# Where the activations' region lies in SBUF: allocated beside xs, at the same remainder modulo 512 bytes

## The chip, the cores and the metric

The kernel runs on one core of a Trainium2 chip. The metric is the device time of one execution in microseconds (us). Runs are compared by their median; the kernel before takes 947.79 us (three runs, 947.37 to 948.18).

## The reference, cut to what matters

A two-layer encoder trunk works on x, 256 positions by 1024 features, in float32. Each layer runs a SwiGLU block, a mixer and a second SwiGLU block, each behind an RMS norm and added back to x:

```python
def swiglu(h, w_gu, w_down):
    g, u = jnp.split(h @ w_gu, 2, axis=-1)
    return (jax.nn.silu(g) * u) @ w_down

for l in range(DEPTH):                     # DEPTH = 2, D_MODEL = 1024, D_FF = 2816
    x = x + 0.5 * swiglu(rmsnorm(x, ffn1_norm[l]), ffn1_w_gu[l], ffn1_w_down[l])
    ...                                    # mix: gated MLP and differential attention, or MLA and GQA
    x = x + mix
    x = x + 0.5 * swiglu(rmsnorm(x, ffn2_norm[l]), ffn2_w_gu[l], ffn2_w_down[l])
```

The four SwiGLU blocks hold most of the arithmetic: per block a gate-and-up product (1024 to 2 x 2816) and a down product (2816 to 1024).

## The kernel before

Features lie along the 128 partitions, positions along the free axis. Every float32 operand of the large products is cut into two float32r parts, a high part and the remainder (hi and lo). A 1 MB piece of weights is loaded by DMA into one of four raw tiles; ScalarE (or VectorE) copies it to a hi tile and VectorE subtracts to make the lo tile. There are six hi and six lo tiles of 1024 elements a partition, used in turn.

Three groups of activations live in SBUF for the products:

- **xs** (KT x 2 x N elements, 8 x 2 x 256): the normed input, hi part (256 columns) and lo part (256 columns) side by side for each of the eight slices of 128 features. Written by `scaled`, read by the gate-and-up products and by the mixers' input products.
- **region** (11264 elements a partition): in a SwiGLU block it holds hs, the 22 slices of the activations, again 256 columns hi and 256 columns lo each (`hs = Arena(region)(FT, 2, N)`). In a mixer it holds the mixer's output os_ and the transposed queries and keys.
- **region32** (5472 elements a partition): float32 intermediates of the mixers.

Two shapes of product do most of the work. In `wide`, a pair of matmuls, the weights are stationary and the activations move: 512 columns (hi and lo) against the hi weights, then 256 columns (hi alone) against the lo weights.

```python
c = T.matmul(b, lhsT=wh, rhs=flat(x2), start=first, stop=False)
c += T.matmul(b[:, 1, :], lhsT=wl, rhs=x2[:, 0, :], start=False, stop=last)
```

The gate-and-up loop runs `wide` over xs with four PSUM banks in rotation (two pairs of gate and up). The down loop runs `wide` over hs in region with two banks in turn: for the last block, the seventh output slice has one bank, and the eighth slice goes through `dense` instead. `dense` is three matmuls (hi with hi, hi with lo, lo with hi). In `out_product`, the mixers' output product, and in that eighth slice, the moving operand of `dense` is 256 columns of region. In `block`, the mixers' input product, the roles are turned: 128 columns of xs are stationary and up to 512 columns of weights move.

The order of all instructions is chosen once, while the kernel is built, by a list scheduler (`Program.schedule`) from costs and dependencies; dependencies are kept by tile name and offset within a tile. Where a tile lies in SBUF is no input to it. Tiles are placed by the pool in the order in which `keep` is called. In the built program the byte addresses within a partition are:

| tile | start before | modulo 512 | start after | modulo 512 |
|---|---|---|---|---|
| hi, lo (all twelve) | 76928 to 121984 | 128 | the same | 128 |
| region | 126080 | 128 | 157984 | 288 |
| region32 | 171136 | 128 | 126080 | 128 |
| gx | 193024 | 0 | 147968 | 0 |
| ident, ones, onesr | 201472 to 202496 | 256 | 156416 to 157440 | 256 |
| xs | 203040 | 288 | 203040 | 288 |

A slice of hs or xs is 2048 bytes, the lo half starts 1024 bytes into it, and 128 columns of weights are 512 bytes, so every operand of `wide` begins at the same remainder modulo 512 as its tile.

Of the kernel before, what the change touches and what calls it, by code (L numbers as in the profile page):

```python
# [12 lines left out]
F32R = mybir.dt.float32r  # L13
# [8 lines left out]
N = 256  # L22
KT = D // P
# [12 lines left out]
ARENA, ARENA32 = 11264, 5472  # L36
# [315 lines left out]
def trunk_kernel(ctx: ExitStack, tc: tile.TileContext, a: dict, out: bass.AP):  # L352
# [20 lines left out]
    def keep(nm, *shape, dt=F32):  # L373
        return sb.tile([P, *shape], dt, name=nm)
# [40 lines left out]
    banks = [ps.tile([P, 512], F32, name=f"bank{k}") for k in range(8)]  # L415
    bank = Taken("bank", Kind(banks, SPARE, True, MOST[0]))
    aux = Taken("aux", Kind(banks, SPARE, True, MOST[1]))
    region, region32 = keep("region", ARENA, dt=F32R), keep("region32", ARENA32)

    def flat(z):  # L420
        return z.rearrange("p a b -> p (a b)")
# [142 lines left out]
        return tp[:w]  # L564


    xs = keep("xs", KT, 2, N, dt=F32R)
    rr_, rb, acc, acc2 = keep("rr", 2), keep("rb", N), keep("acc", N), keep("acc2", 2, N, dt=F32R)
    rr = [rr_[:, h:h + 1] for h in range(2)]

# [587 lines left out]
```

## Time and profile before

| | |
|---|---|
| median of three runs | 947.79 us |
| the profiled execution's own time | 947.75 us |
| its span, from the first to the last instruction | 946.0 us |
| TensorE matmul (PE), busy | 939.6 us, 99% of the span |
| VectorE (DVE), busy | 724.0 us, 77% |
| ScalarE (ACT), busy | 548.4 us, 58% |
| granted TensorE clock | 1.000 |

Every instruction is recorded through one helper, so all lines read L285; the groups are told apart by tiles. A matmul's row names out<-moving,stationary: `bank<-region,hi` streams columns of region past hi weights. Buffer numbers are left out, so region32 is shown as region too; the float32r forms with hi and lo are region's alone. The times of matmuls overlap: the modelled end of one lies behind the start of the next, so the pace of a stream is read from the starts of its instructions, not from their mean durations.

### The profile page before, as it was taken

To read this page: it belongs to the slowest core of one execution; us is meant where nothing else is said; L and a number is where in the kernel's file an instruction comes from. 1 tells how busy PE (TensorE), PEld (TensorE's weight loads), DVE (VectorE), ACT (ScalarE), POOL (GpSimd) and SP (SyncE) were. 2 spreads that over 40 slices of the span, in tenths; PEclk is the share of its full clock that TensorE was granted. 3 is DMA by queue.
4 is the path that set the end of the run, shared out by engine and by line. 5 is a ranking of instruction groups with operands and counts; after the bars stand their busy time and mean duration, and the time that the engine had idled before them with its cause. 6 is when DMAs were issued, how large, how long until landed. Compare 5 with 4: busy or idle time off the path is not lost.

```text
span 946.0 us, 14528 instructions
## 1 busy us (share of the span) xinstructions
PE 939.6 (99%) x5564; PEld 827.1 (87%) x5564; DVE 724.0 (77%) x1326; ACT 548.4 (58%) x938; POOL 29.4 (3%) x57
## 2 busy tenths in 40 slices
PE   9999999999999999999999999999999999999998
PEld 8888888888899888888888888888989988888887
DVE  7997776579989878866588887756888698887642
ACT  7765655446856656554465656544587566565430
POOL 0920000000000000000000000000000000000000
PEclk9999999999999999999999999999999999999999
DMA  8675555543355555555555555554412355555520
GB/s 334 258 267 178 188 201 191 178 178 134 106 207 177 184 193 203 178 182 191 195 182 187 185 202 192 178 185 162 178 55 85 110 186 196 180 192 205 191 102 22
DMA packets 26422, 167.83 MB, mean 177 GB/s; under 512 B 2929, under 2 KB 5105, under 8 KB 7025
## 3 DMA queue, kind: packets, MB, share of 16 engines
q1 hardware_dynamic: 26352, 166.92, 50.0%
q8 instruction: 43, 0.70, 0.3%
q14 instruction: 27, 0.21, 0.1%
HBM read 165.86 MB, written 1.05 MB: 176 GB/s over the span
## 4 chain that ended last, share of the span: by engine, by line
PE 97%; DVE 1%; ACT 1%; DMA 0%; issue 0%; SPq 0%; ACTq 0%
PE bank L285 97%; DVE t L285 0%; ACT t L285 0%; DMA raw<-in_gu 0%; DVE sm L285 0%; ACT hi L285 0%; DVE region L285 0%; DVE lo L285 0%; ACT L285 0%; DVE hi L285 0%; DVE ssg L285 0%; DVE gx L285 0%; SPq L285 0%; DVE ssc L285 0%; DVE rc L285 0%
## 5 line engine op out<-in xcount | busy, mean ns | idle before, releaser
L285 DVE TENSOR_TENSOR lo<-raw,hi 128x1024 fp32r<-128x1024 f32 (+2 forms) x318 | 382.4, 1204 | 165.9 <-ACT hi L285 161.0
L285 ACT ACTIVATE hi<-raw 128x1024 fp32r<-128x1024 f32 (+3 forms) x310 | 322.6, 1043 | 306.1 <-PE bank L285 193.2
L285 PE MATMUL bank<-xs,hi 128*128 128x512 f32 x1408 | 490.8, 393 | 0.4 <-ACT hi L285 0.4
L285 PE MATMUL bank<-xs,lo 128*128 128x256 f32 x1408 | 394.8, 280 | 0.0
L285 PEld LDWEIGHTS bank<-xs,hi 128*128 128x128 f32 x1408 | 265.4, 189 | 59.1 <-ACT hi L285 0.7
L285 PE MATMUL bank<-region,hi 128*128 128x512 f32 (+1 forms) x982 | 296.6, 364 | 0.0
L285 PEld LDWEIGHTS bank<-xs,lo 128*128 128x128 f32 x1408 | 265.3, 188 | 0.7 <-DVE lo L285 0.7
L285 PE MATMUL bank<-region,lo 128*128 128x256 f32 x832 | 234.0, 281 | 0.0
L285 PEld LDWEIGHTS bank<-region,hi 128*128 128x128 f32 x982 | 174.9, 189 | 32.0
L285 PEld LDWEIGHTS bank<-region,lo 128*128 128x128 f32 x832 | 157.6, 189 | 0.0
L285 ACT ACTIVATE t<-bank 128x256 f32<-128x256 f32 (+1 forms) x201 | 76.5, 400 | 39.4 <-PE bank L285 38.4
L285 PE MATMUL bank<-hi,xs 128*128 128x512 f32 (+2 forms) x256 | 78.6, 381 | 0.0
L285 DVE TENSOR_TENSOR t<-bank,t 128x256 f32<-128x256 f32 x176 | 67.3, 420 | 0.4 <-ACT t L285 0.4
L285 DVE TENSOR_TENSOR t<-t,rb 128x512 f32<-128x512 f32 x88 | 60.3, 689 | 1.2
L285 PEld LDWEIGHTS bank<-hi,xs 128*128 128x128 f32 x256 | 47.1, 188 | 8.7
L285 DVE SCALAR_TENSOR_TENSOR gx<-bank,gx 128x256 f32<-128x256 f32 (+1 forms) x71 | 28.4, 450 | 28.7 <-PE bank L285 28.6
L285 PE MATMUL bank<-lo,xs 128*128 128x512 f32 (+2 forms) x128 | 48.0, 375 | 0.0
L285 DVE TENSOR_TENSOR t<-t,t 128x256 f32<-128x256 f32 (+2 forms) x108 | 45.9, 428 | 0.1
L285 ACT ACTIVATE t<-t 128x256 f32<-128x256 f32 (+2 forms) x98 | 39.0, 406 | 3.1 <-DVE t L285 3.1
L285 DVE TENSOR_TENSOR region<-t,region 128x256 fp32r<-128x256 f32 (+2 forms) x92 | 39.1, 430 | 1.1 <-ACT region L285 1.1
L285 ACT ACTIVATE region<-t 128x256 fp32r<-128x256 f32 (+1 forms) x89 | 35.5, 404 | 1.6 <-DVE t L285 1.4
L285 ACT ACTIVATE xs<-gx 128x256 fp32r<-128x256 f32 x48 | 24.0, 500 | 10.8 <-DVE gx L285 9.7
(129 smaller groups left out, 467.4 us busy)
## 6 DMA issues: line engine op xcount, KB each, us to landing
raw<-in_gu SPq DMA_DIRECT2D x86, 1024.0 KB, 4.8
raw<-in_dn SPq DMA_DIRECT2D x44, 1024.0 KB, 4.8
raw<-in_ev_in SPq DMA_DIRECT2D x10, 1024.0 KB, 4.8
raw<-in_ev_out SPq DMA_DIRECT2D x4, 1024.0 KB, 4.9
raw<-in_od_out SPq DMA_DIRECT2D x4, 1024.0 KB, 4.7
raw<-in_gu SPq DMA_DIRECT2D x8, 256.0 KB, 4.6
raw<-in_od_q SPq DMA_DIRECT2D x2, 1024.0 KB, 5.0
raw<-in_od_c SPq DMA_DIRECT2D x2, 832.0 KB, 4.3
```

Source lines behind the costliest of these rows:

```text
L285: r = fn(*map(real, args), **{k: real(v) for k, v in kw.items()})
```

## The change

`region` is no longer allocated ahead of `region32` but just ahead of `xs`. Its size, its contents and every instruction that uses it stay; the addresses change as in the table above. On every engine the built program has the same instructions in the same order.

```diff
@@ -415,7 +415,7 @@
     bank = Taken("bank", Kind(banks, SPARE, True, MOST[0]))
     aux = Taken("aux", Kind(banks, SPARE, True, MOST[1]))
-    region, region32 = keep("region", ARENA, dt=F32R), keep("region32", ARENA32)
+    region32 = keep("region32", ARENA32)
 
     def flat(z):
@@ -564,7 +564,8 @@
         return tp[:w]
 
 
-    xs = keep("xs", KT, 2, N, dt=F32R)
+
+    region, xs = keep("region", ARENA, dt=F32R), keep("xs", KT, 2, N, dt=F32R)
     rr_, rb, acc, acc2 = keep("rr", 2), keep("rb", N), keep("acc", N), keep("acc2", 2, N, dt=F32R)
```

## Rows read from the trace of the kernel before

**Rows 1.** The page: busy time by engine, and the chain that ended last.

```profile
PE 939.6 (99%) x5564; PEld 827.1 (87%) x5564; DVE 724.0 (77%) x1326; ACT 548.4 (58%) x938; POOL 29.4 (3%) x57
...
PE 97%; DVE 1%; ACT 1%; DMA 0%; issue 0%; SPq 0%; ACTq 0%
```

**Rows 2.** Windows: four down stretches, two gate-and-up stretches, the end.

```profile
core 0: us, PE busy (x) PEld busy (x) DVE busy (x) ACT busy (x) POOL busy (x), PEclk, DMA share, GB/s
130.34:192.51 62.17, 62.17 (x354) 53.95 (x353) 38.68 (x56) 29.22 (x40) 0.00 (x0) 1.00 0.53 187
410.55:472.72 62.17, 62.17 (x354) 53.95 (x353) 38.68 (x56) 29.21 (x40) 0.00 (x0) 1.00 0.53 187
594.99:657.16 62.17, 62.17 (x354) 53.92 (x353) 38.77 (x56) 29.21 (x40) 0.00 (x0) 1.00 0.52 180
879.70:934.10 54.40, 54.40 (x311) 47.20 (x309) 28.48 (x39) 19.66 (x23) 0.00 (x0) 1.00 0.34 120
...
296.15:410.55 114.40, 114.40 (x662) 100.69 (x661) 93.43 (x154) 69.58 (x124) 0.00 (x0) 1.00 0.54 190
479.20:594.99 115.79, 115.79 (x670) 101.96 (x669) 94.00 (x153) 69.39 (x125) 0.00 (x0) 1.00 0.54 188
...
925.00:950.00 25.00, 17.18 (x119) 15.75 (x117) 3.85 (x8) 1.05 (x1) 0.00 (x0) 0.95 0.06 21
```

**Rows 3.** Groups by form on PE: out<-moving,stationary, shapes, xcount, busy us, mean ns.

```profile
L285 PE MATMUL bank<-xs,hi 128*128 128x512 f32 x1408 | 490.8, 393 | 0.4 <-ACT hi L285 0.4
L285 PE MATMUL bank<-xs,lo 128*128 128x256 f32 x1408 | 394.8, 280 | 0.0
L285 PE MATMUL bank<-region,hi 128*128 128x512 f32 x682 | 241.1, 399 | 0.0
L285 PE MATMUL bank<-region,lo 128*128 128x256 f32 x832 | 234.0, 281 | 0.0
...
L285 PE MATMUL bank<-region,hi 128*128 128x256 f32 x300 | 55.5, 286 | 0.0
...
L285 PE MATMUL bank<-region 64*128 64x256 f32 x96 | 10.2, 290 | 0.2 <-DVE region L285 0.2
```

**Rows 4.** Timeline of PE, gate-and-up: first and last of 98 pairs; start, duration.

```profile
339.83 0.39 PE L285 MATMUL bank<-xs,hi 128*128 128x512 f32 x1
...
373.80 0.39 PE L285 MATMUL bank<-xs,hi 128*128 128x512 f32 x1
```

**Rows 5.** Timeline of PE, down with two banks: first and last of 96 pairs.

```profile
414.78 0.40 PE L285 MATMUL bank<-region,hi 128*128 128x512 f32 x1
...
448.70 0.40 PE L285 MATMUL bank<-region,hi 128*128 128x512 f32 x1
```

**Rows 6.** Timeline of PE, last block's seventh slice, one bank: 21 pairs.

```profile
926.33 0.40 PE L285 MATMUL bank<-region,hi 128*128 128x512 f32 x1
...
933.75 0.40 PE L285 MATMUL bank<-region,hi 128*128 128x512 f32 x1
```

**Rows 7.** Timeline of PE, even mixer's input product: seven threes of 512 columns.

```profile
201.13 0.63 PE L285 MATMUL bank<-hi,xs 128*128 128x512 f32 x2
...
206.03 0.63 PE L285 MATMUL bank<-hi,xs 128*128 128x512 f32 x2
```

**Rows 8.** Timeline of PE, last block's eighth slice: twenty threes of 256 columns.

```profile
934.34 0.28 PE L285 MATMUL bank<-region,lo 128*128 128x256 f32 x1
...
941.54 0.28 PE L285 MATMUL bank<-region,lo 128*128 128x256 f32 x1
```

**Rows 9.** Groups by form: VectorE and ScalarE writing hs, on ScalarE the hi tiles.

```profile
L285 DVE TENSOR_TENSOR region<-t,region 128x256 fp32r<-128x256 f32 x88 | 36.7, 421 | 1.1 <-ACT region L285 1.1
L285 ACT ACTIVATE region<-t 128x256 fp32r<-128x256 f32 x87 | 34.6, 401 | 1.6 <-DVE t L285 1.4
L285 ACT ACTIVATE hi<-raw 128x1024 fp32r<-128x1024 f32 x294 | 311.0, 1060 | 295.2 <-PE bank L285 186.2 <-issue 103.2 <-ACT hi L285 2.7
```

## The prediction

> **What bounds the kernel now.** I read the page first, then the windows of single stages, then the groups by form, and last the timeline of TensorE, which carries the argument. The page shows TensorE busy 939.6 us of a 946.0 us span, and the chain that ended last lies on it for 97% [rows 1]. So nearly every nanosecond taken from the pace of the matmul stream is taken from the end. [...]
>
> The pace is not the same everywhere, and the busy share hides that. A gate-and-up step and a down step are the same pair of matmuls, 512 moving columns against hi and 256 against lo, with the same count of columns. The starts in the timeline give each one's pace. Gate-and-up moves xs: (373.80 - 339.83) / 98 = 346.6 ns a pair [rows 4]. Down moves region: (448.70 - 414.78) / 96 = 353.3 ns a pair [rows 5]. [...] The difference of 6.7 ns is small and steady, in stretches in which TensorE waits for nobody.
>
> **What differs between the two streams.** By the addresses in the built program, xs begins at remainder 288 modulo 512 and region at 128; the weights of both begin at 128. The other difference is the number of PSUM banks: four in rotation for gate-and-up, two for down. Three more stretches help to separate these.
>
> - The seventh slice of the last block runs the same pairs over region into one bank: (933.75 - 926.33) / 21 = 353.3 ns [rows 6]. Two banks or one make no difference.
> - The even mixer's input product has the roles turned: the weights (remainder 128) move, xs (288) is stationary. Seven threes take 206.03 - 201.13 = 4.90 us, 233.3 ns for one matmul of 512 columns [rows 7].
> - The last block's eighth slice moves 256 columns of region (128): twenty threes take 941.54 - 934.34 = 7.20 us, 120.0 ns for one [rows 8].
>
> The last two add up to 233.3 + 120.0 = 353.3 ns, just the pair of the down stretch, though their stationary operands lie at 288 and 128 and their banks change in other ways. So everything that moves columns from remainder 128 fits one set of prices, whatever the stationary operand and the banks. Only xs, which moves from 288, is faster. I conclude that the remainder of the moving operand sets the 6.7 ns. That is inferred from stretches that differ in more than one thing; no run here has changed the address alone.
>
> **The change part by part.** It moves tiles and no instruction, so nothing is added, removed or reordered on any engine, and no wait is new.
>
> 1. *Down pairs over region.* After the change, hs begins at 288, with the weights at 128 as before: the address remainders of the gate-and-up stream. There are 682 such pairs (the 512-column form of region with hi [rows 3]): 176 in each of three blocks, 154 in the last. I price each at the pace of xs: 682 x (353.3 - 346.6) = 682 x 6.7 = 4.57 us. By stretch that is 1.18 us off each 62.17 and 1.03 us off the 54.40 [rows 2]. All of it is on the path. What could come late instead is the feed of weights; but gate-and-up already runs at 346.6 ns with VectorE at 93.4 of 114.4 us [rows 2], and in down VectorE has more room, 38.7 of 62.2. ScalarE's 1060 ns copies of hi have most of their idle time behind TensorE (186.2 us waiting for a bank's reader to finish [rows 9]), so the tiles wait for TensorE and not the reverse.
>
> 2. *256-column matmuls of region outside the pairs.* There are 300 with hi and 832 - 682 = 150 with lo [rows 3], 450 in all, in the two output products and the eighth slice. The pair's rows do not say which of its two matmuls is the shorter from 288. One end: it is all the 256-column one, which would fall from 120.0 to 113.3 ns and give 450 x 6.7 = 3.0 us more. The other end: the 256-column one becomes dearer while the 512-column one more than pays for it. The mean durations of the forms are 393 against 399 ns for 512 columns and 280 against 281 for 256 [rows 3]: six of the seven nanoseconds sit in the 512-column matmul. A loss of 2.5 ns on each, half of what lies between the two 256-column means of region (281 and 286), would be 1.1 us. I take zero, which is nearest to the row of 280 against 281, and keep -3.0 and +1.1 for the range.
>
> 3. *The other tiles.* region32, gx, ident, ones and onesr shift by 45056 bytes, 88 x 512, so they keep their remainder. I cost them at nothing; if absolute position mattered, the eight slices of xs and the twelve weight tiles, which all lie elsewhere, would not run at one pace over 98 pairs. Region is also an operand of 96 matmuls in the mixers' attention [rows 3]; at 6.7 ns either way that is 0.6 us, and they are short, with VectorE and ScalarE work between them. I take zero.
>
> 4. *Writers.* ScalarE and VectorE write hs while TensorE reads xs, now at the same remainders. No row shows such a write slowing the stream: hi and lo tiles, at 128, are written beside region at 128 all through rows 5, with VectorE busy 38.7 of 62.2 us; in rows 6, at the end, it is busy 3.85 of 25 us and ScalarE 1.05 [rows 2]; the pace is the same. I take zero; its price is among the rivals.
>
> The sum is 4.57 us. Against the profiled execution: 946.0 - 4.6 = 941.4 us of span, with 947.75 - 946.0 = 1.75 us outside it, 943.2 us. The median, 947.79, is 0.04 above that execution, so 943.2 stands for the median too.
>
> **The rivals.**
>
> *No change (947.8 us).* The four-bank rotation, not the address, makes gate-and-up fast, and down stays at 353.3 ns. For it: the only fast stretch is also the only one with four banks changing at every pair. Against it: one and two banks cost the same [rows 5, 6], and prices from stretches with other bank patterns add up to the same pair [rows 7, 8]. [...]
>
> *Part of the gain is given back (944.6 us).* Writes of hs meet reads of xs at the same remainder. The writes take 36.7 + 34.6 = 71.3 us [rows 9]; in that time TensorE does 71.3 / 0.3466 = 206 pairs of gate-and-up, and if each falls back to 353.3 ns, 206 x 6.7 = 1.4 us of the 4.6 are lost. Against it stands point 4.
>
> *More than the sum (940.2 us).* The gain sits in the 256-column matmul, and the 450 others get it too, 3.0 us. Against it stand the durations in point 2.
>
> *Slower (956.2 us).* A start at 288, which is 32 bytes past a multiple of 64, costs TensorE time, and xs runs fast only because four banks hide more than that. Down, with two banks, then shows the cost: taking the step seen here, 6.7 ns for 512 columns and half of it for 256, it is 682 x (6.7 + 3.35) + 450 x 3.35 = 6.9 + 1.5 = 8.4 us. It decides as soon as a down pair takes more than 353.3 ns. For it: no stretch moves columns from 288 with two banks or one. Against it: the stream at 288 is the fastest here, and the banks have shown no price.
>
> **How the numbers follow.** Forecast 0.72, giving-back 0.06, more than the sum 0.07, no change 0.11, slower 0.04. The likeliest gives 943.2 us. Its own spread (point 2's small differences, point 3's 0.6, runs that differ by 0.4 either way) is about 942.2 to 944.4. The range reaches to 945.6 above, which takes in giving-back, and to 941.2 below, which takes in part of the case of 940.2; no change, slower and the rest below are left out, 0.20 together. A difference of 0.2%, 1.9 us, is about what a measurement of this kernel can tell from no change. Forecast, giving-back and more than the sum are faster by more than that: 0.85. No change is 0.11, slower 0.04.
>
> **What would show it right or wrong.** In the profile of the changed kernel the down stretches should have pairs 346.6 ns apart, so about 61.0 us instead of 62.17 and 53.4 instead of 54.40; the 512-column form of region with hi should have a mean near 393 ns. Gate-and-up pairs should stay at 346.6 (347 or more would be giving-back), the eighth slice's matmuls at 120.0 (113 would be more than the sum), the input products at 233.3. If the down pairs stay at 353.3 while region lies at 288, my reading of the remainder is wrong, and the banks are next to be tried.

## The result and the profile after

The changed kernel takes 942.35 us (median of six runs, 942.05 to 942.80) against 947.63 us for the kernel before beside it: a ratio of 0.9941, 95% interval 0.9930 to 0.9951. The forecast was 943.2 us, 4.6 us less than before; measured are 5.3 us less. The profiled execution has a span of 940.6 us instead of 946.0.

The windows of the same stretches as in [rows 2], four down and two gate-and-up, with the same columns:

```profile
130.23:191.25 61.02, 61.02 (x355) 53.73 (x354) 38.68 (x56) 29.24 (x40) 0.00 (x0) 1.00 0.55 190
408.92:469.93 61.01, 61.01 (x354) 53.72 (x353) 38.66 (x56) 29.23 (x40) 0.00 (x0) 1.00 0.53 189
592.19:653.20 61.01, 61.01 (x354) 53.73 (x353) 38.72 (x56) 29.27 (x40) 0.00 (x0) 1.00 0.53 183
875.49:928.87 53.38, 53.38 (x310) 46.99 (x309) 28.46 (x39) 19.71 (x23) 0.00 (x0) 1.00 0.35 122
294.52:408.92 114.40, 114.40 (x663) 100.73 (x661) 93.43 (x154) 69.61 (x124) 0.00 (x0) 1.00 0.55 190
476.40:592.19 115.79, 115.79 (x670) 101.98 (x669) 93.98 (x153) 69.42 (x125) 0.00 (x0) 1.00 0.54 188
```

The down stretches went from 62.17 to 61.01 us and from 54.40 to 53.38: 1.15 + 1.16 + 1.16 + 1.02 = 4.5 us. Gate-and-up has not moved by a hundredth. TensorE is as fully busy as before (61.01 of 61.01 us in the second down stretch) and the granted clock is the same, 1.00; the stream itself has become denser. The first and the last of 98 down pairs in the timeline of TensorE (start, duration), against [rows 5]:

```profile
412.73 0.39 PE L285 MATMUL bank<-region,hi 128*128 128x512 f32 x1
...
446.70 0.39 PE L285 MATMUL bank<-region,hi 128*128 128x512 f32 x1
```

(446.70 - 412.73) / 98 = 346.6 ns a pair, the pace of xs. The groups by form, against [rows 3]:

```profile
L285 PE MATMUL bank<-region,hi 128*128 128x512 f32 x682 | 236.6, 392 | 0.0
L285 PE MATMUL bank<-region,lo 128*128 128x256 f32 x832 | 232.8, 280 | 0.0
...
L285 PE MATMUL bank<-region,hi 128*128 128x256 f32 x300 | 54.8, 284 | 0.0
...
L285 PE MATMUL bank<-region 64*128 64x256 f32 x96 | 10.2, 291 | 0.2 <-DVE region L285 0.2
```

The 512-column form went from a mean of 399 to 392 ns, the mean of xs. The rest of the gain is in the 256-column matmuls outside the pairs. The eighth slice of the last block, 22 threes against the twenty of [rows 8] (the first row is the matmul just ahead of them, the last of the seventh slice):

```profile
928.76 0.28 PE L285 MATMUL bank<-region,lo 128*128 128x256 f32 x1
...
936.50 0.28 PE L285 MATMUL bank<-region,lo 128*128 128x256 f32 x1
```

That is 7.74 us / 66 = 117.3 ns instead of 120.0. The mixers' stretches, which hold the other 384 of these matmuls, in the windows of the kernel before:

```profile
192.51:288.27 95.76, 95.75 (x582) 82.68 (x581) 85.75 (x215) 63.55 (x109) 0.00 (x0) 1.00 0.44 155
657.16:757.42 100.26, 99.19 (x717) 91.48 (x715) 80.98 (x229) 67.05 (x139) 0.00 (x0) 1.00 0.31 109
```

and after:

```profile
191.25:286.64 95.39, 95.39 (x582) 82.33 (x581) 85.53 (x215) 63.36 (x108) 0.00 (x0) 1.00 0.45 155
653.20:753.22 100.02, 98.97 (x716) 91.30 (x715) 80.89 (x229) 66.94 (x139) 0.00 (x0) 1.00 0.31 109
```

They are 0.4 and 0.2 us shorter. The starts place most of the even mixer's part in the output product. Its longest unbroken stretch, 34 threes, before and after:

```profile
275.91 0.28 PE L285 MATMUL bank<-region,lo 128*128 128x256 f32 x1
...
288.15 0.28 PE L285 MATMUL bank<-region,lo 128*128 128x256 f32 x1
...
274.55 0.28 PE L285 MATMUL bank<-region,lo 128*128 128x256 f32 x1
...
286.52 0.28 PE L285 MATMUL bank<-region,lo 128*128 128x256 f32 x1
```

12.24 us became 11.97, 120.0 ns for one matmul became 117.4. In the other long stretches of the output products, read in the same way, the gain is smaller, 1.3 ns for one: fifty threes of the odd mixer went from 757.30 - 739.30 = 18.00 us to 753.11 - 735.30 = 17.81, eighteen of the even mixer from 6.48 to 6.41. With 66 x 2.7 ns = 0.2 us in the eighth slice, 4.5 + 0.6 + 0.2 = 5.3 of the 5.4 us of span are placed.

### The profile page after: what moved, and what is told of

The parts are those of the page before. It is cut to its first block, busy times and chain, and to the rows that moved or that the text cites. A ratio compares the mean times of both kernels' runs of the same rounds, so it can differ in the third digit from the quotient of the medians.

```text
span 940.6 us, 14528 instructions
## 1 busy us (share of the span) xinstructions
PE 934.3 (99%) x5564; PEld 825.5 (88%) x5564; DVE 724.2 (77%) x1326; ACT 548.2 (58%) x938; POOL 27.2 (3%) x57
## 4 chain that ended last, share of the span: by engine, by line
PE 97%; DVE 1%; ACT 1%; DMA 0%; issue 0%; SPq 0%; ACTq 0%
PE bank L285 97%; DVE t L285 0%; ACT t L285 0%; DMA raw<-in_gu 0%; DVE sm L285 0%; ACT hi L285 0%; DVE region L285 0%; DVE lo L285 0%; ACT L285 0%; DVE hi L285 0%; DVE ssg L285 0%; DVE gx L285 0%; SPq L285 0%; DVE ssc L285 0%; DVE rc L285 0%
## 5 line engine op out<-in xcount | busy, mean ns | idle before, releaser
L285 PE MATMUL bank<-region,hi 128*128 128x512 f32 (+1 forms) x982 | 291.4, 359 | 0.0
```

The lines of the kernel that those rows point to most:

```text
L285: r = fn(*map(real, args), **{k: real(v) for k, v in kw.items()})
```

## The experiments

All move tiles or the place of data within a tile; the contents and the arithmetic stay. Up to the scans each run has, on every engine, the instructions of the changed kernel in the same order, so there addresses alone differ. In the scans TensorE's order is still the same, but a few instructions of VectorE and ScalarE change places; in the versions with two starts the order shifts on TensorE too. The edits are shown against the changed kernel or the kernel before, whichever is nearer. In what follows d is the start of the moving operand minus that of the stationary operand, modulo 512 bytes. Before the change d was 160 for gate-and-up and 0 for down; the change made it 160 for both. For the mixers' input products, whose moving operand is the weights, it was 352 and stayed so. Each scan was timed once, so its trace is read and not its time.

**xs moved as well, both at 128.**

```diff
+    region, xs = keep("region", ARENA, dt=F32R), keep("xs", KT, 2, N, dt=F32R)
     region32 = keep("region32", ARENA32)
```

> region and xs both begin at remainder 128, like the weights; from the changed kernel (942.35 us) only addresses differ. Theory A (the moving operand's own start decides): gate-and-up pairs slow from 346.6 to 353.3 ns as the down pairs go back to 353.3; 1408 x 6.7 = 9.4 us and 682 x 6.7 = 4.6 us and about 0.7 us for the 450 others, together 957.1 us. Theory B (the relation of moving to stationary decides): the same here, since the difference is zero. Theory C (four banks in rotation keep gate-and-up fast and something else helped the down pairs): gate-and-up stays at 346.6, down returns to 353.3, 947.6 us.

954.88 us (three runs at 954.78 to 955.07, one at 952.28), a ratio of 1.0065 (1.0051 to 1.0080) to the kernel before. The timeline of TensorE in gate-and-up, first and last of 98 pairs, then the even mixer's input product, first and last of seven threes, then twenty threes of the last block's eighth slice:

```profile
339.67 0.40 PE L285 MATMUL bank<-xs,hi 128*128 128x512 f32 x1
...
374.30 0.40 PE L285 MATMUL bank<-xs,hi 128*128 128x512 f32 x1
...
202.83 0.62 PE L285 MATMUL bank<-hi,xs 128*128 128x512 f32 x2
...
207.59 0.61 PE L285 MATMUL bank<-hi,xs 128*128 128x512 f32 x2
...
941.57 0.28 PE L285 MATMUL bank<-region,lo 128*128 128x256 f32 x1
...
948.77 0.28 PE L285 MATMUL bank<-region,lo 128*128 128x256 f32 x1
```

Gate-and-up has 34.63 us / 98 = 353.4 ns with all four banks in rotation: the banks are out, and with them the rival of no change. But the input products, whose moving operand still lies at 128, went from 233.3 to 4.76 us / 21 = 226.7 ns. Neither theory A nor the plain form of B said that. Over the 288 matmuls of this shape (192 with hi, 96 with lo) that makes, as an estimate, 288 x 6.6 ns = 1.9 us, most of what the time is under the 957.1 expected. The eighth slice kept 7.20 us / 60 = 120.0 ns.

**The weights at 288 too.**

```diff
-    raws_, his, los = Turns("raw", RAW, SUB), Turns("hi", RING, PIECE, F32R), Turns("lo", RING, PIECE, F32R)
+    raws_ = Turns("raw", RAW, SUB)
...
     warm = keep("warm", 1)
+    his, los = Turns("hi", RING, PIECE, F32R), Turns("lo", RING, PIECE, F32R)
```

> hi and lo tiles also begin at remainder 288, with region and xs at 288: moving and stationary operands have the same remainder, none is at 128. Theory A: down and gate-and-up pairs stay at 346.6 ns, and the input products, whose moving operand is now at 288, fall from 233.3 to about 229 ns for 512 columns; 288 of those matmuls x 4 ns = 1.2 us less, 941.2 us. Theory B: equal remainders are slow, so both streams take 353.3 ns: 1408 x 6.7 + 682 x 6.7 = 14 us more, about 957 us.

950.22 us, ratio 1.0027 (1.0016 to 1.0038); its twelve runs lie in two groups, 948.3 to 948.9 and 951.5 to 952.7. So a moving start of 288 is not fast in itself (353.3 ns a pair in the first window below): theory A falls. Nor is d = 0 always slow. Its windows, a gate-and-up and a down stretch twice:

```profile
294.13:410.72 116.59, 116.59 (x663) 101.07 (x661) 93.91 (x154) 69.76 (x124) 0.00 (x0) 1.00 0.54 185
410.72:472.91 62.19, 62.19 (x355) 53.90 (x353) 38.67 (x55) 29.22 (x40) 0.00 (x0) 1.00 0.53 189
479.51:595.31 115.80, 115.80 (x671) 102.10 (x670) 93.97 (x153) 69.38 (x125) 0.00 (x0) 1.00 0.54 188
595.31:656.32 61.01, 61.01 (x355) 53.79 (x353) 38.70 (x56) 29.21 (x40) 0.00 (x0) 1.00 0.52 183
```

With 330, 176, 334 and 176 pairs these are 353.3, 353.4, 346.7 and 346.6 ns. One program with one d runs whole stretches at either pace. In both blocks of these windows the down stretch had the pace of the gate-and-up before it. Of the other two, the first block's down stretch was fast, 61.01 us / 176 = 346.6 ns, and the fourth block's gate-and-up slow: 649 matmuls in 114.00 us, against 647 in as long a window of the second block's and 660 of the third's.

**region at 256, and region at 160.** The tile warm (32 bytes) is placed behind region instead of ahead; in the second, warm and region go ahead of region32.

> region begins at 256 (a multiple of 64), xs stays at 288, the weights at 128. Theory A, in the form that multiples of 64 are slow: down pairs 353.3 ns, 947.6 us. Theory B (equality with the stationary operand's remainder is what is slow): 256 differs from 128, so down pairs stay at 346.6 ns, 942.4 us.

> region begins at 160, 32 past a multiple of 64 but not at xs's remainder modulo 512 (288); the weights stay at 128. Theory A in the form of 64 bytes: down pairs 346.6 ns, 942.4 us. If it has to be the remainder of xs modulo 512 itself: down pairs 353.3 ns, 947.6 us. Theory B by the distance from the weights: 32 is another distance than 160, anything between 346.6 and 353.3 ns.

945.84 us, ratio 0.9982 (0.9973 to 0.9991), and 941.78 us, ratio 0.9936 (0.9923 to 0.9949). The second down stretch of each in the windows, region at 256 first:

```profile
410.04:471.83 61.79, 61.79 (x355) 54.16 (x354) 38.67 (x56) 29.21 (x40) 0.00 (x0) 1.00 0.54 188
```

```profile
408.47:469.49 61.02, 61.02 (x355) 54.09 (x354) 38.66 (x56) 29.23 (x40) 0.00 (x0) 1.00 0.54 191
```

Over 176 pairs that is 351.1 ns at d = 128, between the two paces and as neither theory had it, and 346.7 at d = 32. The same remainder as xs isn't needed.

**All shifted by 32: weights at 288, region and xs at 320.** The edit is that of the run with the weights at 288, with a tile of 32 bytes behind them. Theory B2, in this expectation and the next ones, is what the runs so far left of B: the pace depends on d, and not only on whether d is zero.

> As the run with the weights at 288, but region and xs lie 32 bytes further, at 320: d = 32 for all pairs, and every moving operand of a pair starts at a multiple of 64. Theory B2: pairs 346.7 ns as in the run with region at 160 and the weights at 128, so the distance alone decides; 942 us or less. Theory A (multiples of 64 are slow): 353 ns in both streams, 957 us.

941.81 us in its one run. Gate-and-up and down in the windows:

```profile
294.35:408.76 114.41, 114.41 (x662) 101.41 (x661) 93.38 (x154) 69.57 (x124) 0.00 (x0) 1.00 0.55 190
408.76:469.77 61.01, 61.01 (x354) 54.09 (x353) 38.65 (x56) 29.22 (x40) 0.00 (x0) 1.00 0.54 190
```

346.7 and 346.6 ns with the moving operands at a multiple of 64, where theory A asked for 353. The moving operand's own start does not decide in these runs. The third block of the first scan below makes it sharper: there hs begins at 320 too, with the weights at 128 (d = 192), and its pairs take 353.3 ns. The two streams with a start of 320 differ in where the operands lie to each other. That d alone sets the pace, wherever both lie, was tried at two distances only, 0 and 32, and d = 0 has two paces, 353.3 and 346.7 ns.

**The scans.** Region gets 56 elements more, and each of the four SwiGLU blocks puts hs at another offset in it.

```diff
-        hs = Arena(region)(FT, 2, N)
+        hs = view(region[:, shift:shift + FT * 2 * N], (FT, 2, N))
...
-    ffn(*f10, norm[1])
+    ffn(*f10, norm[1], 16)
```

> A scan inside one run: the activations of the four SwiGLU blocks begin 64, 128, 192 and 224 bytes past the weights' remainder, xs 384 past it (address only; the contents are the same). Let d be the start of the moving operand minus that of the stationary one, modulo 512. Theory B2 (d decides; so far pairs took 353.3 ns at d = 0, 351.1 at 128, 346.7 at 32 and 160): pairs differ from block to block with d, the second block near 351, the fourth and perhaps the others at 346.7; the input products at d = 128 take neither 227.8 (d = 0) nor 233.5 ns (d = 352) for certain. Theory A (own start, multiples of 64 are slow): the blocks at 64, 128 and 192 past 128 are multiples of 64 and all near 353, the fourth (352) at 346.7, gate-and-up (0) at 353.

> The same scan with d = 224, 288, 352 and 384 for the four blocks and d = 128 for gate-and-up, input products at d = 384. Theory B2: gate-and-up near 351 ns as the down pairs were at d = 128 before; the blocks again by d. Theory A (multiples of 64): the first three blocks start at 352, 416 and 480, 32 past multiples of 64, so 346.7; the fourth starts at 0, so 353.

> The rest of the scan: d = 320, 416, 448 and 480 in the four blocks, gate-and-up and input products at d = 256. If the pace repeats every 256 bytes, pairs take 353.3 ns at 320 (as at 64), 346.7 at 416 (as at 160), 353.3 at 448 (as at 192), 346.7 at 480 (as at 224), and 353.3 at 256 (as at 0, with input products near 227.8). If the 512 bytes of one weight load set it, 256 is an ordinary distance and the others need not repeat.

> d = 480 again, in the first, third and fourth block, and d = 96 in the second block and in gate-and-up, with input products at d = 416. If 480 is slow by itself, all three blocks take about 353 ns a pair. If at 480 a stretch falls into one of two paces, as at 0 and 256, the three differ or take 346.7. If the pace repeats every 256 bytes, d = 96 is like 352 (350.0 ns).

The down stretches of these four runs in their windows (176 pairs in the first three of a run, 154 in the fourth). d = 64, 128, 192, 224:

```profile
131.90:194.08 62.18, 62.18 (x354) 54.23 (x353) 38.67 (x55) 29.20 (x40) 0.00 (x0) 1.00 0.53 188
413.38:475.18 61.80, 61.80 (x355) 54.18 (x354) 38.66 (x55) 29.21 (x40) 0.00 (x0) 1.00 0.53 187
598.99:661.17 62.18, 62.18 (x354) 54.01 (x353) 38.75 (x55) 29.21 (x40) 0.00 (x0) 1.00 0.52 180
885.08:938.47 53.39, 53.39 (x311) 46.92 (x309) 28.44 (x38) 19.68 (x23) 0.00 (x0) 1.00 0.35 121
```

d = 224, 288, 352, 384:

```profile
132.94:193.96 61.02, 61.02 (x354) 53.63 (x353) 38.64 (x55) 29.24 (x40) 0.00 (x0) 1.00 0.54 190
412.95:473.96 61.01, 61.01 (x354) 54.08 (x353) 38.64 (x55) 29.22 (x40) 0.00 (x0) 1.00 0.54 190
597.78:659.39 61.61, 61.61 (x355) 53.79 (x354) 38.75 (x55) 29.22 (x40) 0.00 (x0) 1.00 0.52 181
883.09:937.16 54.07, 54.07 (x310) 47.39 (x309) 28.46 (x38) 19.65 (x23) 0.00 (x0) 1.00 0.35 120
```

Two gate-and-up stretches at d = 256 (330 and 334 pairs), and down at d = 320, 416, 448, 480:

```profile
131.58:193.76 62.18, 62.18 (x354) 54.17 (x353) 38.68 (x55) 29.20 (x40) 0.00 (x0) 1.00 0.54 187
295.64:412.24 116.60, 116.60 (x663) 101.07 (x661) 93.95 (x154) 69.78 (x124) 0.00 (x0) 1.00 0.54 187
412.24:473.27 61.03, 61.03 (x355) 53.73 (x354) 38.66 (x55) 29.25 (x40) 0.00 (x0) 1.00 0.54 189
479.85:595.64 115.79, 115.79 (x670) 102.09 (x669) 93.94 (x153) 69.36 (x125) 0.00 (x0) 1.00 0.54 188
595.64:657.82 62.18, 62.18 (x355) 54.01 (x353) 38.69 (x56) 29.22 (x40) 0.00 (x0) 1.00 0.52 180
879.60:934.00 54.40, 54.40 (x311) 47.25 (x309) 28.50 (x39) 19.68 (x23) 0.00 (x0) 1.00 0.34 120
```

d = 480, 96, 480, 480:

```profile
132.14:194.32 62.18, 62.18 (x355) 54.00 (x354) 38.64 (x55) 29.19 (x40) 0.00 (x0) 1.00 0.54 187
413.49:475.09 61.60, 61.60 (x354) 53.66 (x353) 38.64 (x55) 29.21 (x40) 0.00 (x0) 1.00 0.54 188
598.56:660.74 62.18, 62.18 (x354) 54.00 (x353) 38.63 (x55) 29.20 (x40) 0.00 (x0) 1.00 0.52 180
884.01:937.40 53.39, 53.39 (x310) 46.92 (x309) 28.44 (x38) 19.68 (x23) 0.00 (x0) 1.00 0.35 122
```

By these windows and the readings above, a pair takes:

| d | pair, ns | d | pair, ns |
|---|---|---|---|
| 0 | 353.3 or 346.7 | 256 | 353.3 or 346.7 |
| 32 | 346.7 | 288 | 346.6 |
| 64 | 353.3 | 320 | 353.3 |
| 96 | 350.0 | 352 | 350.1 |
| 128 | 351.1 | 384 | 351.1 |
| 160 | 346.6 | 416 | 346.8 |
| 192 | 353.3 | 448 | 353.3 |
| 224 | 346.7 (twice) | 480 | 353.2 to 353.3 (three times), 346.7 (once) |

Seven of eight rows repeat after 256 bytes. 224 against 480 may be a further case of two paces; two stretches at 224 don't settle it. With the weights at 128, d is a multiple of 64 just where the start is one, so the scans alone would leave theory A nearly standing. Against it go d = 96, 352 and 480, starts that it calls fast, the two fast stretches at d = 256, a start that it calls slow, and the 351.1 ns at 128 and 384. What decides are the two runs with the weights at 288. Only d = 0 and 32 were read with the weights at 288 as well as at 128, and the 346.7 ns at d = 0 stood there alone: with the weights at 128 the stretches read at d = 0 were slow, the four before at 353.3 ns and, with both at 128, the second block's gate-and-up at 353.4 and its down at 353.3. The expectation of 346.7 at d = 480 was missed; in the repeat two of three stretches missed it again.

The expectations ask for the input products too. Seven threes, read as in [rows 7], give for one matmul of 512 columns 226.7 to 228.6 ns at d = 256, 232.4 at 128 and at 384, 232.9 at 480 and 234.3 at 416. So 0 (226.7 ns with both at 128) and 256 are fast for them, and no other distance that was tried is.

**A version that uses it: two starts for xs.** The input products ran at 226.7 ns at d = 0, against 233.3 at the 352 of the kernel before, and the pairs at 346.7 ns at d = 32, so xs is written and read at one offset for the SwiGLU blocks and at another for the mixers; region is at d = 32.

```diff
+    xa, region = keep("xs", KT * 2 * N + 8, dt=F32R), keep("region", ARENA, dt=F32R)
+    xm, xs = (view(xa[:, o:o + KT * 2 * N], (KT, 2, N)) for o in (0, 8))
...
-        split(xs[:, k, 0, :], xs[:, k, 1, :], x[:, k, :], g)
+        z = xm if n in (1, 4) else xs
+        split(z[:, k, 0, :], z[:, k, 1, :], x[:, k, :], g)
```

> The weights stay at 128; region and the gate-and-up reads of xs are at 160 (d = 32), and for the mixers' input products xs is written and read 32 bytes earlier, at 128 (d = 0). Theory B2: pairs 346.7 ns, 256-column matmuls about 117, input products 227.8 instead of 233.5 ns for 512 columns; against the run with region at 160 (941.8 us) that is 274 x 5.7 = 1.6 us less, 940.2 us. If input products are fast only when the pairs are slow, or the like: 941.8 us, no change. The two starts share words at their borders, so the built order of a few instructions shifts; that could cost some tenths.

941.67 us, ratio 0.9932 (0.9918 to 0.9945): not the 940.2 expected. A second version has the offsets 0 for xs (d = 288) and 56 elements for the mixers' copy (d = 0). It ran on one chip with a repeat of the kernel with region at 160.

> As the run with two starts, but the gate-and-up copy of xs begins at the tile's start (d = 288, paces of 346.7 ns in the scan) and the mixers' copy 224 bytes further (d = 0); region at d = 32. The words at the borders of slices are shared in the mixers' copy instead of the other. If the 0.9 us lost in the first gate-and-up stretch of the earlier run came from those shared words and not from the addresses, that stretch goes back from 125.75 to about 124.85 us, the mixers keep their 94.0 and 99.3 us, and the time is 940.3 us, a ratio of 0.992 to the kernel before. If the addresses did it, 941.7 us.

> The kernel with region at 160 once more, beside the run with two starts on one chip: 941.8 us, a ratio of 0.9936, with the input products at 233.5 ns.

940.36 us (940.20 to 940.44), ratio 0.9922 (0.9908 to 0.9935), and 942.60 us (941.92 to 943.89), ratio 0.9947 (0.9933 to 0.9961). The first gate-and-up stretch and the two mixers in the windows, second version with two starts, then the repeat:

```profile
5.19:130.27 125.08, 125.04 (x707) 110.26 (x707) 109.67 (x185) 83.67 (x150) 28.01 (x49) 1.00 0.68 244
191.28:285.24 93.96, 93.96 (x583) 82.11 (x582) 85.68 (x215) 62.89 (x107) 0.00 (x0) 1.00 0.45 157
651.79:751.10 99.31, 98.22 (x717) 90.93 (x716) 80.86 (x229) 66.74 (x138) 0.00 (x0) 1.00 0.31 110
```

```profile
5.18:131.03 125.85, 125.10 (x706) 109.28 (x707) 109.48 (x185) 83.44 (x150) 28.55 (x49) 1.00 0.67 243
192.05:287.21 95.16, 95.16 (x583) 82.16 (x581) 85.50 (x214) 63.31 (x108) 0.00 (x0) 1.00 0.44 155
653.80:753.46 99.66, 98.60 (x717) 90.95 (x716) 80.76 (x229) 66.77 (x138) 0.00 (x0) 1.00 0.32 109
```

The repeat's 942.60 us is 0.8 above the 941.8 expected. The mixers give 1.2 + 0.35 = 1.55 us, about the 1.6 worked out. The first stretch is another matter: the kernel with region at 160 took 124.85 us in it in its first profile and 125.85 in the repeat, so a microsecond there comes and goes with the execution. The shared words that I held responsible in the first version are therefore neither shown nor excluded. The second version is faster than the repeat beside it by more than the runs of either scatter. Beside the changed kernel itself it wasn't run; their ratios to the kernel before, 0.9922 and 0.9941, have intervals that overlap.

## Why the prediction was right, and where its reason was wrong

- *What bounds the kernel*: right. 5.3 of the 5.4 us of span are placed in the pace of the matmul stream, and the time fell by 5.3 us. One row is misnamed on the way: the 186.2 us of [rows 9] are waits for matmuls, which write the bank and read the hi tile, not for a bank's reader. That the tiles wait for TensorE stands.
- *Point 1, 682 pairs at the pace of xs, 4.57 us*: right, 4.5 us measured and 346.6 ns a pair.
- *Point 2, the 450 other matmuls at zero*: the term that was mis-sized. It gave about 0.8 us (0.6 in the mixers, 0.2 in the eighth slice), inside the bound of 3.0 but not the zero to which the row of 280 against 281 ns pointed. That row mixes the pairs with these streams; its mean went from 281 to 280 ns where the starts of the eighth slice went from 120.0 to 117.3, so here the mean of modelled durations didn't carry over, and the starts would have to be read in such a stream.
- *Points 3 and 4, other tiles and writers*: nothing seen. The 96 attention matmuls of [rows 3] kept their 10.2 us, gate-and-up its 114.40 and 115.79 us.
- *"The remainder of the moving operand sets the 6.7 ns"*: wrong, and the forecast didn't need it. The down pairs got the operand starts of the gate-and-up pairs, moving and stationary, so either reading gave the same time. A start at 288 with weights elsewhere would not have been safe, as the run with the weights at 288 shows, where such pairs took 353.3 ns in one block and 346.7 in another. The sum that led to it, 233.3 + 120.0 = 353.3 [rows 5, 7, 8], joined two distances (352 and 0) and met the pair's price by coincidence: with xs at 128 too the same two prices add up to 226.7 + 120.0 = 346.7, beside pairs of 353.4.
- *The rivals*: no change (four banks) fell with xs at 128, where four banks ran at 353.4 ns. Slower fell with the result. More than the sum came in part, 0.8 of its 3.0 us. Giving-back isn't seen: gate-and-up kept its windows of 114.40 and 115.79 us.

With the weights at 128, a down pair takes 346.7 ns at a distance of 32 between its operands' addresses and 353.3 at 64. What makes it so no run here shows.

## What to carry to other kernels

When TensorE is busy for the whole stretch, compare the start-to-start pace of streams with equal shapes; here a 2% difference between two of them (346.6 against 353.3 ns a pair), invisible in the busy share, was worth 0.6% of the kernel for a move of two lines. Look then at the distance between the moving and the stationary operand's addresses, not at either alone, and try it per shape: a distance of 0, at which the 512-and-256 pairs ran at their slowest pace in the kernel before (353.3 ns), was among the two best for the input products' streams of 512 (226.7 ns, as at 256). Two streams that differ in several things may add up by chance; one run that moves a single address tells more than the sum.

## What the runs showed of the hardware that I had not expected

- The pair's pace by distance takes few values, 346.7, 350.0, 351.1 and 353.3 ns for 768 columns, and repeats after 256 bytes in seven of eight cases. All but the distances 0 and 32 were read with the weights at 128 alone.
- At d = 0, 256 and 480 a stretch runs at 346.7 or at 353.3 ns and keeps to it, and both are seen in one execution of one program. All four down stretches of the kernel before (d = 0) stood at 353.3 ns in its profile. What chooses is open.
- The input products' 512-column matmuls have a scale of their own: about 227 to 229 ns at d = 0 and 256, 232.4 to 234.3 at the other distances that were tried.
